# Two seven-product pairs instead of three, and splits with the weights' priority, in a two-layer fp32 block

## The chip, the core and the metric

The kernel runs on one core of a Trainium2 chip (trn2). The metric is device time in microseconds (us), median of the runs. PE is the matmul engine and PEld its weight loads, DVE the vector engine, ACT the scalar engine, POOL GpSimd, SP the engine that issues the DMAs here.

## The reference

Two layers over 256 rows of 2048 numbers, all in fp32. Each layer has a mixer (a gated linear recurrence, differential attention and latent attention side by side) and a feed-forward part. Only the second half of a layer matters here:

```
h = rmsnorm(x, g_ffn[l])
x = x + (silu(h @ w_gate[l]) * (h @ w_up[l])) @ w_down[l]
```

`w_gate` and `w_up` are 2048 x 5632, `w_down` is 5632 x 2048. The mixer's code is not touched.

## The kernel before, in words

Each product of fp32 matrices is made of three matmuls on numbers that are split in two: `hi` is the value rounded to the matmul's format (fp32r), `lo` the rest, and the product is hi x hi + hi x lo + lo x hi (`mm3`, lines 231 to 236). So each weight that arrives by DMA in a `wraw` buffer (6 of them, 512 KB each over 128 partitions) is first copied to `whi` by ACT (line 228) and then subtracted to `wlo` by DVE (line 229); of these there are 3 each.

The feed-forward part goes over 11 blocks f of 512 columns, in groups of 4, 4 and 3. For each f, `gate_up` computes gate and up for both halves of the 256 rows; there are 22 such calls in the two layers. After a group, its rows of `w_down` are multiplied in a stage of its own.

The 16 k-tiles of 128 rows are taken as 8 pairs. One pair is a 2 x 2 by 2 x 2 block product: two halves of the rows by two k-tiles, times two k-tiles by (gate, up). The first `NORD` pairs (5) are ordinary: 8 block products, 24 matmuls of 512 columns. The rest (3) use a scheme of the Strassen kind with 7 block products, 21 matmuls. For it, DVE makes sums of the weights, V and W (lines 340 to 343), in two more `wraw` buffers, and G, U, V and W are split into `arena` by ACT (lines 338, 339, 346, 348) and DVE (lines 344, 345, 347, 349). The arena holds two sets of such splits, at `p % 2 * SET`, so that one pair's are written while the other's are read. Sums of x for these pairs are made once a layer by `build_xS` into `xSh` and `xSl`.

PSUM has eight banks here: five of `acc`, three of `aux`. The seven-product part needs all five `acc` (C11, C22, C21, C12, P1) and all three `aux` (P5, P7, P6, lines 324 and 325).

When the last pair is done, DVE and ACT form silu(gate) * up in `sil` (lines 354 to 380). The down product needs it transposed and split. That is `hidden()`: two steps, each of four transposes on PE into an `aux` bank (line 393), a copy to `hTh` by ACT (line 399) and a subtraction to `hTl` by DVE (line 400). The steps are run by `tick()` beside the next call of `gate_up`, so its transposes stand in PE's order behind that call's third and fourth pair:

```
def hidden(sil=sil, h=h, lo=lo):
    yield 2
    for k in range(0, 4, 2):
        ps = transposed([0, 128, 256, 384], ...)
        split_scaled(fl(h[:, k:k + 2]), fl(lo[:, k:k + 2]), ps, None)
        yield
add(hidden())
```

PE runs in the order of the program text. The order on DVE, ACT and SP is made by a scheduler, which puts what stands under `tc.high_priority(offset=AHEAD)` ahead of the rest where both could go; the weights' splits, the sums and silu stand under it, `hidden()` does not. Every engine then works through its own row strictly in order.

Below, pair 0 to pair 7 are the eight pairs of a call.

Of the kernel before, what the change touches and what calls it, by code (L numbers as in the profile page):

```python
# [21 lines left out]
P = 128  # L22
D = 2048
T = 256
NT = 2
# [8 lines left out]
AHEAD = 100000  # L34
WIDTH = 2
STEPS = 2

NORD = 5
ARENA1, ARENA2 = 14504, 2816
MAGIC = 12582912.0  # L40
TWO_PI = 2.0 * math.pi
# [16 lines left out]
def body(ctx: ExitStack, tc: tile.TileContext, x_in, pos_in, pvec_in, lamv_in, cst_in, w_in, w_r, w_i, w_q_b,  # L58
# [26 lines left out]

    xSh = xt_p.tile([P, KD // 2 - NORD, 4, P], F32R, name="xSh")
    xSl = xt_p.tile([P, KD // 2 - NORD, 4, P], F32R, name="xSl")
    ar_p = pool("arena")
# [48 lines left out]
    A_ON = A_RG + 1024 + 1536  # L137
    A_DQ = A_QT

    SET = 7168  # L140
    A_SIL = ARENA1
    A_U = A_SIL + 1024

# [48 lines left out]
    def run(gen, ticks=None):  # L192
        for i, _ in enumerate(gen):
            if ticks is None or i < ticks:
                tick()
# [36 lines left out]
    def mm3(ps, a, b, start, stop):  # L232

        nc.tensor.matmul(ps, a[0], b[0], start=start, stop=False)  # L234
        nc.tensor.matmul(ps, a[0], b[1], start=False, stop=False)  # L235
        nc.tensor.matmul(ps, a[1], b[0], start=False, stop=stop)  # L236
# [61 lines left out]
    def gate_up(wg, wu, rs, sil):  # L298
# [3 lines left out]
        fl = lambda v: v.rearrange("p a b -> p (a b)")  # L302
# [7 lines left out]
        def xp(k, t):  # L310
            return xTh[:, k, t * P:(t + 1) * P], xTl[:, k, t * P:(t + 1) * P]

        for p in range(NORD):
            ks = (2 * p, 2 * p + 1)
            hl = [load_split(w[2 * p * P:(2 * p + 2) * P], 2, (512,)) for w in (wg, wu)]
            for s, t in ((0, 0), (1, 1), (0, 1), (1, 0)):
                hi, lo = hl[s]
                for j, k in enumerate(ks):
                    mm3(bank[s, t], xp(k, t), (hi[:, j], lo[:, j]), p == 0 and j == 0,
                        (s, t) == (1, 1) and p == NORD - 1 and j == 1)  # L320
            yield
# [4 lines left out]
        n = KD // 2  # L326
        for p in range(NORD, n):
            ks = (2 * p, 2 * p + 1)
            a = p % 2 * SET
            G, U = (load(w[2 * p * P:(2 * p + 2) * P], 2, (512,)).rearrange("p (a b) -> p a b", a=2)  # L330
                    for w in (wg, wu))
            V, W = (wraw_p.tile([P, CHUNK], F32, name="wraw").rearrange("p (a b) -> p a b", a=2) for _ in range(2))
            gh, gl = at(a, 2, 512), at(a + 1024, 2, 512)
            uh, ul = at(a + 2048, 512), at(a + 2560, 512)
            vh, vl = at(a + 3072, 2, 512), at(a + 4096, 2, 512)
            wh, wl = at(a + 5120, 2, 512), at(a + 6144, 2, 512)
            with tc.high_priority(offset=AHEAD):
                nc.scalar.copy(fl(gh), fl(G))  # L338
                nc.scalar.copy(uh, U[:, 1])
                tt(V[:, 0], U[:, 0], G[:, 0], ALU.subtract)  # L340
                tt(V[:, 1], U[:, 1], U[:, 0], ALU.subtract)  # L341
                tt(W[:, 0], U[:, 1], V[:, 0], ALU.subtract)  # L342
                tt(W[:, 1], G[:, 1], W[:, 0], ALU.subtract)  # L343
                tt(fl(gl), fl(G), f_(fl(gh)), ALU.subtract)  # L344
                tt(ul, U[:, 1], f_(uh), ALU.subtract)  # L345
                nc.scalar.copy(fl(vh), fl(V))  # L346
                tt(fl(vl), fl(V), f_(fl(vh)), ALU.subtract)
                nc.scalar.copy(fl(wh), fl(W))  # L348
                tt(fl(wl), fl(W), f_(fl(wh)), ALU.subtract)  # L349
            first, end = p == NORD, p == n - 1  # L350
            q = p - NORD
            S = [(xSh[:, q, i], xSl[:, q, i]) for i in range(4)]
            mm3(P1, xp(ks[0], 0), (gh[:, 0], gl[:, 0]), first, end)
            if end:
                with tc.high_priority(offset=AHEAD):
                    nc.scalar.copy(sil[1], P1)
            mm3(C11, xp(ks[1], 0), (gh[:, 1], gl[:, 1]), False, end)
            if end:
                with tc.high_priority(offset=AHEAD):
                    tt(sil[0], sil[1], C11, ALU.add)  # L360
                    nc.scalar.activation(sil[0], sil[0], AF.Silu, scale=rs[:, 0:1])
            mm3(C12, S[3], (uh, ul), False, end)
            mm3(P5, S[0], (vh[:, 0], vl[:, 0]), first, end)
            mm3(P7, S[2], (vh[:, 1], vl[:, 1]), first, end)
            mm3(P6, S[1], (wh[:, 0], wl[:, 0]), first, end)
            if end:
                with tc.high_priority(offset=AHEAD):
                    tt(u2, sil[1], P6, ALU.add)
                    tt(u3, u2, P7, ALU.add)
            mm3(C21, xp(ks[1], 1), (wh[:, 1], wl[:, 1]), False, end)  # L370
            if end:
                with tc.high_priority(offset=AHEAD):
                    tt(sil[1], u3, C21, ALU.add)
                    nc.scalar.activation(sil[1], sil[1], AF.Silu, scale=rs[:, 1:2])
                    tt(u2, u2, P5, ALU.add)
                    tt(u2, u2, C12, ALU.add)
                    tt(u3, u3, P5, ALU.add)
                    tt(u3, u3, o22, ALU.add)
                    for t, u in ((0, u2), (1, u3)):
                        nc.vector.scalar_tensor_tensor(sil[t], u, rs[:, t:t + 1], sil[t], ALU.mult, ALU.mult)  # L380
            yield
# [4 lines left out]
    def aux():  # L386
        return aux_p.tile([P, 512], F32, name="aux")

    def transposed(dsts, srcs):

        ps = aux()
        for d, s in zip(dsts, srcs):
            nc.tensor.transpose(ps[:, d:d + P], s, ident)  # L393
        return ps

    def split_scaled(hi, lo, src, g):

        if g is None:
            i = nc.scalar.copy(hi, src)
            nc.vector.tensor_tensor(lo, src, hi.bitcast(F32), ALU.subtract)  # L400
        else:
            i = nc.scalar.activation(hi, src, AF.Copy, scale=g)
            nc.vector.scalar_tensor_tensor(lo, src, g, hi.bitcast(F32), ALU.mult, ALU.subtract)  # L403
        return i
# [161 lines left out]
    def layer(l, rs):  # L566
# [3 lines left out]
        fl = lambda v: v.rearrange("p b t -> p (b t)")  # L570
# [231 lines left out]
        for i in range(4):  # L802
            h = ht_p.tile([P, 4, T], F32R, name="hTh")
            lo = ht_p.tile([P, 4, T], F32R, name="hTl")
            for j in range(4):

                k = (list(range(10, 16)) + list(range(6)) + list(range(6, 10)))[i * 4 + j]
# [148 lines left out]
        for f0, f1 in ((0, 4), (4, 8), (8, 11)):  # L956
            hT = []
            for f in range(f0, f1):
                sil = [at(A_SIL + t * 512, 512) for t in range(NT)]
                fs = slice(f * 512, (f + 1) * 512)  # L960
                run(gate_up(w_gate[l][:, fs], w_up[l][:, fs], rs[0], sil))
                h = ht_p.tile([P, 4, T], F32R, name="hTh")
                lo = ht_p.tile([P, 4, T], F32R, name="hTl")

                def hidden(sil=sil, h=h, lo=lo):
                    yield 2
                    for k in range(0, 4, 2):
                        ps = transposed([0, 128, 256, 384],
                                        [sil[t][:, (k + j) * P:(k + j + 1) * P] for j in range(2) for t in range(NT)])
                        split_scaled(fl(h[:, k:k + 2]), fl(lo[:, k:k + 2]), ps, None)  # L970
                        yield
                add(hidden())
                for j in range(4):
                    hT.append((h[:, j, :], lo[:, j, :]))
            last = f1 == 11
            if end and last:
                take(F32)
                gf = at(0, D)
                nc.sync.dma_start(gf, g_final.to_broadcast([P, D]))
            for cg in range(2):  # L980
                fin = end and last and cg == 1

                def ev(s, t, g, ps):
                    c = cg * 1024 + g * 512
                    nc.vector.tensor_tensor(x[:, t, c:c + 512], x[:, t, c:c + 512], ps, ALU.add)
                    if last:
                        sumsq(ss[:, t, cg * 2 + g:cg * 2 + g + 1], x[:, t, c:c + 512])
                    if end and last and cg == 0:
                        nc.vector.tensor_tensor(x[:, t, c:c + 512], x[:, t, c:c + 512], gf[:, c:c + 512], ALU.mult)
                    if fin and g == 1:  # L990
                        finish(t, ss, gf)
                run(gemm(lambda k: hT[k],
                         [(w_down[l][f0 * 512:f1 * 512, cg * 1024:(cg + 1) * 1024], [(0, 512), (512, 512)])],
                         [[k] for k in range(4 * (f1 - f0))], ev, last=3 if fin else 0))
                drain()
                if last and not end:
                    add(xT_steps("g_mix", l + 1, cg * 8, cg * 8 + 8))
# [62 lines left out]
```

## Time and profile before

| | |
|---|---|
| median of 3 runs | 2241.07 us (2236.26 to 2241.4) |
| the profiled execution | 2241.19 us, span 2239.4 us |
| mean granted clock of PE | 0.974 |
| PE busy | 2108.8 us (94%), 10104 matmuls |
| weight loads busy | 1761.2 us (79%) |
| DVE busy | 1545.2 us (69%) |
| ACT busy | 1136.2 us (51%) |
| HBM | 387.30 MB read, 174 GB/s over the span |

A matmul's end is modelled in the trace and reaches into the next one, so PE's pace is read from one start to the next. A wait is shown in brackets behind the instruction that waited, with what ended it.

### The profile page before, as it was taken

How to read it: one execution, taken by the hardware profiler on the slowest of the kernel's cores; microseconds unless marked ns; L12 is line 12 of the kernel's file. 1: busy time of each engine (PE TensorE's matmuls, PEld its weight loads, DVE VectorE, ACT ScalarE, POOL GpSimd, SP SyncE). 2: the span in 40 equal slices, each digit the busy share in tenths (PEclk: the TensorE clock that was granted, in tenths of full speed). 3: DMA queues.
4: the chain of work that ended last, by engine and by line, in shares of the span. 5: the costliest groups of instructions: out<-in, count | busy, mean ns of one | idle time of the engine just before them, and what ended most of it. 6: DMA issues, size and time to landing. Idle time of an engine off the chain costs nothing.

```text
span 2239.4 us, 27021 instructions
## 1 busy us (share of the span) xinstructions
PE 2108.8 (94%) x10104; PEld 1761.2 (79%) x10104; DVE 1545.2 (69%) x2115; ACT 1136.2 (51%) x1541; POOL 14.9 (1%) x32
## 2 busy tenths in 40 slices
PE   8999999888998889988999999998889988899888
PEld 8899887777887778877898898877778877788776
DVE  5775658777477774777566756587764877648775
ACT  5854656444354443444447545564543554434444
POOL 0000000000000000000000000000000000000000
PEclk9999999999999999999999999999999999999999
DMA  7564555545664555554565645654556645565553
GB/s 240 167 184 132 170 182 160 175 160 170 193 199 162 169 168 190 180 195 150 175 189 159 179 149 163 183 169 151 173 184 191 195 160 160 186 191 191 169 191 133
DMA packets 183220, 391.17 MB, mean 175 GB/s; under 512 B 18960, under 2 KB 36384, under 8 KB 182960
## 3 DMA queue, kind: packets, MB, share of 16 engines
q1 hardware_dynamic: 183040, 389.36, 54.9%
q8 instruction: 79, 1.29, 0.2%
q14 instruction: 53, 0.43, 0.1%
q0 software_dynamic: 48, 0.09, 0.0%
HBM read 387.30 MB, written 2.10 MB: 174 GB/s over the span
## 4 chain that ended last, share of the span: by engine, by line
PE 69%; DVE 17%; DMA 8%; issue 4%; ACT 2%; SPq 0%; DVEq 0%; POOLq 0%; POOL 0%; ACTq 0%
PE acc L235 20%; PE acc L234 20%; PE acc L236 20%; DMA wraw<-in_w_up 5%; DVE wlo L229 4%; PE aux L234 2%; DVE arena L344 2%; PE aux L235 2%; PE aux L236 2%; DVE arena L349 2%; ACT whi L228 1%; PE aux L393 1%; DVE arena L345 1%; DVE wraw L342 1%; DVE wraw L343 1%
## 5 line engine op out<-in xcount | busy, mean ns | idle before, releaser
L229 DVE TENSOR_TENSOR wlo<-wraw,whi 128x1024 fp32r<-128x1024 f32 (+2 forms) x608 | 716.1, 1182 | 451.5 <-ACT whi L228 446.2
L228 ACT CAST whi<-wraw 128x1024 fp32r<-128x1024 f32 (+2 forms) x608 | 618.7, 1019 | 728.4 <-PE acc L236 536.2
L235 PE MATMUL acc<-wlo,xTh 128*128 128x512 f32 (+1 forms) x1200 | 465.7, 388 | 11.3 <-DVE wlo L229 11.2
L234 PE MATMUL acc<-whi,xTh 128*128 128x512 f32 (+1 forms) x1200 | 471.1, 393 | 0.0
L236 PE MATMUL acc<-whi,xTl 128*128 128x512 f32 (+1 forms) x1200 | 463.5, 386 | 0.0
L234 PE MATMUL acc<-whi,hTh 128*128 128x512 f32 (+1 forms) x992 | 388.2, 391 | 0.0
L236 PE MATMUL acc<-whi,hTl 128*128 128x512 f32 (+1 forms) x992 | 384.7, 388 | 0.0
L235 PE MATMUL acc<-wlo,hTh 128*128 128x512 f32 (+1 forms) x992 | 384.4, 387 | 0.0
L235 PEld LDWEIGHTS acc<-wlo,xTh 128*128 128x128 f32 x1200 | 225.5, 188 | 65.7 <-DVE wlo L229 23.0
L234 PEld LDWEIGHTS acc<-whi,xTh 128*128 128x128 f32 x1200 | 225.4, 188 | 43.9 <-ACT whi L228 0.5
L236 PEld LDWEIGHTS acc<-whi,xTl 128*128 128x128 f32 x1200 | 225.3, 188 | 44.1
L234 PEld LDWEIGHTS acc<-whi,hTh 128*128 128x128 f32 x992 | 186.4, 188 | 37.8 <-issue 1.3
L236 PEld LDWEIGHTS acc<-whi,hTl 128*128 128x128 f32 x992 | 186.2, 188 | 37.9
L235 PEld LDWEIGHTS acc<-wlo,hTh 128*128 128x128 f32 x992 | 186.4, 188 | 36.4
L234 PE MATMUL aux<-arena,xSh 128*128 128x512 f32 x198 | 83.1, 420 | 100.6 <-DVE hTl L400 76.0
L234 PEld LDWEIGHTS aux<-arena,xSh 128*128 128x128 f32 x198 | 38.8, 196 | 114.1 <-ACT whi L228 93.2
L234 PE MATMUL acc<-xTh,whi 128*128 128x256 f32 x384 | 111.1, 289 | 1.7 <-ACT whi L228 1.0
L235 PE MATMUL acc<-xTl,whi 128*128 128x256 f32 x384 | 108.8, 283 | 1.6 <-DVE xTl L403 1.6
L236 PE MATMUL acc<-xTh,wlo 128*128 128x256 f32 x384 | 108.6, 283 | 0.5 <-DVE wlo L229 0.5
L346 ACT CAST arena<-wraw 128x1024 fp32r<-128x1024 f32 x66 | 69.3, 1049 | 47.6 <-DVE wraw L341 47.4
L344 DVE TENSOR_TENSOR arena<-wraw,arena 128x1024 fp32r<-128x1024 f32 x66 | 80.7, 1223 | 14.4 <-ACT arena L338 13.8
L348 ACT CAST arena<-wraw 128x1024 fp32r<-128x1024 f32 x66 | 69.4, 1051 | 36.3 <-DVE wraw L343 28.7
(230 smaller groups left out, 2614.5 us busy)
## 6 DMA issues: line engine op xcount, KB each, us to landing
wraw<-in_w_gate SPq DMA_DIRECT2D x176, 512.0 KB, 4.4
wraw<-in_w_up SPq DMA_DIRECT2D x176, 512.0 KB, 4.6
wraw<-in_w_down SPq DMA_DIRECT2D x176, 512.0 KB, 4.3
wraw<-in_w_out SPq DMA_DIRECT2D x64, 512.0 KB, 3.8
wraw<-in_w_in SPq DMA_DIRECT2D x48, 512.0 KB, 4.0
wraw<-in_w_in SPq DMA_DIRECT2D x48, 384.0 KB, 3.2
wraw<-in_w_in SPq DMA_DIRECT2D x32, 416.0 KB, 3.5
arena<-in_w_in SPq DMA_DIRECT2D x16, 384.0 KB, 7.4
```

The lines of the kernel that those rows point to most:

```text
L228: nc.scalar.copy(hi[:, :n], raw[:, :n])
L229: nc.vector.tensor_tensor(lo[:, :n], raw[:, :n], hi[:, :n].bitcast(F32), ALU.subtract)
L234: nc.tensor.matmul(ps, a[0], b[0], start=start, stop=False)
L235: nc.tensor.matmul(ps, a[0], b[1], start=False, stop=False)
L236: nc.tensor.matmul(ps, a[1], b[0], start=False, stop=stop)
L342: tt(W[:, 0], U[:, 1], V[:, 0], ALU.subtract)
L343: tt(W[:, 1], G[:, 1], W[:, 0], ALU.subtract)
L344: tt(fl(gl), fl(G), f_(fl(gh)), ALU.subtract)
L345: tt(ul, U[:, 1], f_(uh), ALU.subtract)
L346: nc.scalar.copy(fl(vh), fl(V))
L348: nc.scalar.copy(fl(wh), fl(W))
L349: tt(fl(wl), fl(W), f_(fl(wh)), ALU.subtract)
```

## The change

Three edits. `NORD` goes from 5 to 6, so 6 pairs are ordinary and 2 use seven products; `xSh` and `xSl` shrink from three entries to two. The transposes and splits of `hidden()` are issued under the weights' priority. The two sets in `arena` begin 64 elements (256 bytes) later.

```diff
-NORD = 5
+NORD = 6
...
-    SET = 7168
+    A_SET, SET = 64, 7168
...
         for p in range(NORD, n):
             ks = (2 * p, 2 * p + 1)
-            a = p % 2 * SET
+            a = A_SET + p % 2 * SET
...
                 def hidden(sil=sil, h=h, lo=lo):
                     yield 2
                     for k in range(0, 4, 2):
-                        ps = transposed([0, 128, 256, 384],
-                                        [sil[t][:, (k + j) * P:(k + j + 1) * P] for j in range(2) for t in range(NT)])
-                        split_scaled(fl(h[:, k:k + 2]), fl(lo[:, k:k + 2]), ps, None)
+                        with tc.high_priority(offset=AHEAD):
+                            ps = transposed([0, 128, 256, 384],
+                                            [sil[t][:, (k + j) * P:(k + j + 1) * P] for j in range(2)
+                                             for t in range(NT)])
+                            split_scaled(fl(h[:, k:k + 2]), fl(lo[:, k:k + 2]), ps, None)
                         yield
                 add(hidden())
```

How DVE's row changes is seen best in the third call of a group, which has the `hidden()` of the second beside it. The numbers in the names count buffers; they differ between the two programs. Before, at the end of the call, with the sums of pair 7 (`wraw_4294`, `wraw_4295`) and then the second `hTl`, behind which the next call's first weights follow:

```order
L340 TENSOR_TENSOR wraw_4294<-wraw_4292,wraw_4290 128x512
L341 TENSOR_TENSOR wraw_4294<-wraw_4292 128x512
L342 TENSOR_TENSOR wraw_4295<-wraw_4292,wraw_4294 128x512
L344 TENSOR_TENSOR arena_3292<-wraw_4290,arena_3292 128x1024
L343 TENSOR_TENSOR wraw_4295<-wraw_4290,wraw_4295 128x512
L345 TENSOR_TENSOR arena_3292<-wraw_4292,arena_3292 128x512
L347 TENSOR_TENSOR arena_3292<-wraw_4294,arena_3292 128x1024
L400 TENSOR_TENSOR hTl_4008<-aux_4164,hTh_4007 128x512
L229 TENSOR_TENSOR wlo_4351<-wraw_4348,whi_4350 128x1024
```

Now, in the middle of the call, with the split of pair 6's V (line 347), the second `hTl`, and then the first weights of pair 5 (`wlo_4196`):

```order
L347 TENSOR_TENSOR arena_3292<-wraw_4238,arena_3292 128x1024
L400 TENSOR_TENSOR hTl_3994<-aux_4150,hTh_3993 128x512
L229 TENSOR_TENSOR wlo_4196<-wraw_4193,whi_4195 128x1024
L342 TENSOR_TENSOR wraw_4239<-wraw_4236,wraw_4238 128x512
L343 TENSOR_TENSOR wraw_4239<-wraw_4234,wraw_4239 128x512
```

The second `hTl` stood behind all three pairs' sums but one split; it now stands inside those of the first of two.

The second place is the start of the first seven-product pair of that call on DVE. Before, it is pair 5 (sums in `wraw_4216`), and `wlo_4137` is the up weights of pair 3:

```order
L344 TENSOR_TENSOR arena_3292<-wraw_4212,arena_3292 128x1024
L340 TENSOR_TENSOR wraw_4216<-wraw_4214,wraw_4212 128x512
L341 TENSOR_TENSOR wraw_4216<-wraw_4214 128x512
L229 TENSOR_TENSOR wlo_4137<-wraw_4134,whi_4136 128x1024
L345 TENSOR_TENSOR arena_3292<-wraw_4214,arena_3292 128x512
```

Now it is pair 6 (sums in `wraw_4238`), with the first `hTl` ahead of it, and `wlo_4166` is the up weights of pair 4:

```order
L400 TENSOR_TENSOR hTl_3994<-aux_4107,hTh_3993 128x512
L344 TENSOR_TENSOR arena_3292<-wraw_4234,arena_3292 128x1024
L340 TENSOR_TENSOR wraw_4238<-wraw_4236,wraw_4234 128x512
L341 TENSOR_TENSOR wraw_4238<-wraw_4236 128x512
L345 TENSOR_TENSOR arena_3292<-wraw_4236,arena_3292 128x512
L229 TENSOR_TENSOR wlo_4166<-wraw_4163,whi_4165 128x1024
```

The split of line 345 has moved ahead of the weights' split.

## Rows read from the trace of the kernel before

**Rows 1.** Page, costliest groups: busy, mean ns | idle before, what ended it.
```profile
L234 PE MATMUL aux<-arena,xSh 128*128 128x512 f32 x198 | 83.1, 420 | 100.6 <-DVE hTl L400 76.0
```
**Rows 2.** Waits of PE: who for whom, us in total, times, longest.
```profile
PE aux L234 <- DVE hTl L400: 76.0, 12, 7.3
PE aux L234 <- ACT whi L228: 24.6, 4, 6.6
PE acc L235 <- DVE wlo L229: 11.2, 17, 1.2
```
**Rows 3.** Timeline of PE, one call: start us, us, instruction, idle before.
```profile
467.29 0.39 PE L236 MATMUL aux<-arena,xSl 128*128 128x512 f32 x1
474.88 0.77 PE L234 MATMUL aux<-arena,xSh 128*128 128x512 f32 x1 [7.21 <-DVE hTl L400]
...
479.20 0.39 PE L235 MATMUL acc<-arena,xTh 128*128 128x512 f32 x1
```
**Rows 4.** Timeline of ACT, the same call.
```profile
461.44 0.58 ACT L399 CAST hTh<-aux 128x512 fp32r<-128x512 f32 x1
```
**Rows 5.** Timeline of DVE, the same call.
```profile
451.71 0.69 DVE L340 TENSOR_TENSOR wraw<-wraw 128x512 f32<-128x512 f32 x1 [0.92 <-DMA wraw<-in_w_up]
...
452.92 1.22 DVE L229 TENSOR_TENSOR wlo<-wraw,whi 128x1024 fp32r<-128x1024 f32 x1
454.06 0.69 DVE L345 TENSOR_TENSOR arena<-wraw,arena 128x512 fp32r<-128x512 f32 x1
454.66 1.22 DVE L229 TENSOR_TENSOR wlo<-wraw,whi 128x1024 fp32r<-128x1024 f32 x1
...
474.05 0.69 DVE L400 TENSOR_TENSOR hTl<-aux,hTh 128x512 fp32r<-128x512 f32 x1
```
**Rows 6.** Windows: us, busy of PE, PEld, DVE, ACT, POOL, PEclk, DMA share, GB/s.
```profile
467.70:474.80 7.10, 0.00 (x0) 0.00 (x0) 7.10 (x11) 3.96 (x5) 0.00 (x0) 0.82 0.62 181
...
627.04:669.02 41.98, 41.78 (x184) 34.27 (x183) 34.43 (x39) 23.90 (x26) 0.00 (x0) 1.00 0.60 187
654.75:669.02 14.27, 14.27 (x64) 11.83 (x63) 13.57 (x17) 9.34 (x11) 0.00 (x0) 1.00 0.67 222
412.55:435.86 23.31, 17.18 (x65) 13.67 (x63) 15.43 (x19) 9.07 (x10) 0.00 (x0) 0.85 0.63 211
...
2141.28:2163.78 22.50, 16.50 (x64) 13.20 (x63) 15.29 (x19) 9.06 (x10) 0.00 (x0) 0.85 0.60 218
474.88:479.20 4.32, 4.32 (x11) 3.41 (x11) 3.61 (x4) 2.09 (x2) 0.00 (x0) 0.51 1.02 377
```
**Rows 7.** Groups by form, DVE and ACT: busy, mean ns of one.
```profile
L229 DVE TENSOR_TENSOR wlo<-wraw,whi 128x1024 fp32r<-128x1024 f32 x508 | 619.0, 1223 | 401.0 <-ACT whi L228 396.4
L344 DVE TENSOR_TENSOR arena<-wraw,arena 128x1024 fp32r<-128x1024 f32 x66 | 80.7, 1223 | 14.4 <-ACT arena L338 13.8
...
L340 DVE TENSOR_TENSOR wraw<-wraw 128x512 f32<-128x512 f32 x66 | 45.5, 690 | 22.4 <-DMA wraw<-in_w_up 22.2
...
L400 DVE TENSOR_TENSOR hTl<-aux,hTh 128x512 fp32r<-128x512 f32 x44 | 30.1, 685 | 0.0
...
L228 ACT CAST whi<-wraw 128x1024 fp32r<-128x1024 f32 x508 | 533.9, 1052 | 632.9 <-PE acc L236 500.9 <-issue 59.8 <-DMA wraw<-in_w_gate 21.1
...
L346 ACT CAST arena<-wraw 128x1024 fp32r<-128x1024 f32 x66 | 69.3, 1049 | 47.6 <-DVE wraw L341 47.4
```
**Rows 8.** Timeline of SP's queue, the same call.
```profile
447.96 0.37 SPq L212 DMA_DIRECT2D wraw<-in_w_up  x1
```
**Rows 9.** Timeline of PE, the same call and one without transposes.
```profile
454.25 0.44 PE L235 MATMUL acc<-wlo,xTh 128*128 128x512 f32 x1
...
644.73 0.39 PE L234 MATMUL acc<-whi,xTh 128*128 128x512 f32 x1
645.31 0.50 PE L235 MATMUL acc<-wlo,xTh 128*128 128x512 f32 x1 [0.20 <-DVE wlo L229]
```
**Rows 10.** Windows, the first call of layer 0.
```profile
342.00:390.00 48.00, 43.12 (x188) 33.55 (x187) 42.41 (x66) 31.31 (x43) 0.00 (x0) 1.00 0.52 163
```

## The prediction

> **What bounds the kernel now.** I read four views, each narrower than the last. The page's table of groups shows which PE group has idle time in front of it: nearly all of PE's idle time, 100.6 us, stands in front of one group, the first of three matmuls of a block product that writes an `aux` bank [rows 1]. The list of waits splits it: 12 waits of up to 7.3 us on `hTl` (line 400) and 4 of up to 6.6 us put down to `whi`; everything else that PE waits for is short, 17 waits on `wlo` with 11.2 us in all [rows 2]. So 16 waits. There are 22 calls of `gate_up`; the first of each of the six groups of f has no `hidden()` of an earlier call beside it, and 22 - 6 = 16. The four on `whi` are the same wait: same line, same place.
>
> The timelines show why. `aux` has three banks. `hidden()` of the call before takes two for its transposes, during the ordinary pairs; the first seven-product pair then wants three (P5, P7, P6). P6 gets the bank of the second transposes, which is free only when the copies to `hTh` and `hTl` have read it. In one such call PE stops after 467.29 and goes on at 474.88 [rows 3]. ACT had written `hTh` at 461.44 [rows 4]; DVE does `hTl` only at 474.05 [rows 5]. Between them DVE is never idle: 7.10 of 7.10 us [rows 6], on sums and splits of pairs 6 and 7, which have the weights' priority, while `hidden()` has none. The first block of rows in the change section says the same: `hTl_4008<-aux_4164` stands behind both pairs' sums. PE waits for a 0.69 us instruction in the wrong place of a queue.
>
> [...]
>
> **The change, part by part.**
>
> *The splits with priority.* They move in DVE's row from behind pair 7's sums to the middle of pair 6's; nothing is added. PE's order is the program's own and stays. What goes is the excess of the stretch of three seven-product pairs: 14.27 us without the wait, 23.31 in the first and 22.50 in the last of the 16 calls with it [rows 6]; all 16 lie between 22.0 and 23.7 and sum to 364.7. So 364.7 - 16 x 14.27 = 136.4 us. [...] Can the splits now hold up something else? Queued behind the second `hTl` on DVE is a `wlo` of pair 5 (`wlo_4196`). Its transposes are issued behind pair 3, `wlo_4196` waits for a buffer that pair 3 frees and is wanted only when pair 4 is done, 24 x 0.2265 = 5.4 us later. Two times 0.69 [rows 7] fits. The first `hTl` stands behind pair 4's first split, which itself waits for pair 2; its transposes run directly behind pair 2. I count no cost.
>
> *One pair with eight block products.* Three matmuls more per call: 22 x 3 x 0.2265 = 15.0 us, all on PE and so all on the path.
>
> [...]
>
> *What DVE and ACT lose and get.* A seven-product pair costs DVE five 512-wide instructions (0.69) and three 1024-wide (1.22), 7.1 us; an ordinary pair two of 1.22, 2.4 [rows 7]. A call without wait holds 34.43 us of DVE work in 41.98 [rows 6]; it comes to about 29.8 in 42.7, and 31.1 with the two `hTl`. DVE has the room on average; this is worth nothing on the path by itself, it is what makes the removed wait stay away: what is late next is only a matter of order.
>
> *The order around pair 4.* Here is the one new wait that I expect. DVE's order puts the sums of the first seven-product pair ahead of an ordinary split. Before, in the call shown, SP issues the up weights of pair 5 at 447.96 [rows 8], DVE starts on them at 451.71 after waiting for the landing, does two sums, and then the `wlo` that PE wants: 452.92 to 454.14 [rows 5]. PE uses it at 454.25 [rows 9], so it is just on time. In a call without transposes it is late: 0.20 recorded at 645.31 [rows 9], where the step from the matmul before is 0.58 in place of 0.2265, and the next one is long too, some 0.27 more than recorded. The second pair of blocks in the change section shows that now `L345` (from its start to the next is 0.60 [rows 5]) stands ahead of that `wlo` too. Everything else slides by one pair alike, with one more set of transposes on PE's side (about 0.3). So 0.3 late, 0.55 us of loss per call: 22 x 0.55 = 12.1 us. Bounds: 0 (the transposes cover it) and 1.2 + 0.27, the longest of the short waits, in every call: 32 us.
>
> *Fewer sums of x.* One of three `build_xS` per layer goes, in each layer's first call, which has short waits of its own: PE idles 48.00 - 43.12 = 4.9 us in its stretch [rows 10]. From 0 to -5 us a layer; I take 0, since the pair that stays first meets the same sums.
>
> *256 bytes.* Splits written into `arena` take 1223 ns on DVE and 1049 on ACT, those into `wlo` and `whi`, at quite other addresses, 1223 and 1052 [rows 7]; PE reads both at 0.2265. Nothing to gain, and two addresses with one speed give no reason for a loss: 0, within 3 ns an instruction.
>
> Sum, against the profiled execution (2241.2 us, span 2239.4; the median of the runs, 2241.07, is the same): 2241.2 - 136.4 + 15.0 + 12.1 = 2131.9, so **2132 us**. Its own range, by the bounds of the order term and a few us for the first calls: 2118 to 2145.
>
> **Rivals.**
>
> *No new wait at all.* The split stays in time everywhere and the first calls get shorter: 2241.2 - 136.4 + 15.0 = 2119.8, less up to 7: 2113 to 2120. For it: a call with transposes shows no wait there today. Against: one without does.
>
> *The up weights become the wait.* Without the 7 us pauses loads have less lead. If their landing is late by another us or two, each call loses 1.5 to 2.5 us at that same `wlo`: 2119.8 + 33 to 55 = 2153 to 2175. For it: `L340` waits for the up weights already. Against: a stretch without wait gets 222 GB/s [rows 6], and behind a wait 377 GB/s flow, so the engines have room.
>
> [...]
>
> *The wait only moves (slower than before).* If DVE, which works through its queue in order, stands at the head with an `hTl` whose transposes PE has not reached, pair 4's `wlo` behind it comes late, PE stops and pays wait and clock again, at pair 4 in place of P6: 16 times the same 8.5 us, and 15.0 for the added products, 2256 us. It decides from (136.4 - 15.0) / 22 = 5.5 us of new loss per call. The same time results if the edit of the priority does nothing, which the rows of the order exclude. Against it: by the order the transposes are issued one pair ahead of need.
>
> **How the numbers follow.** Forecast 0.62, no new wait 0.15, up weights 0.13, clock 0.03, wait moves 0.05, something between 2175 and 2235 0.02. A measurement of this kernel tells about 0.3% (7 us) from no change. All but the fifth are faster; of the fifth 0.02 I count as no change. Faster 0.94, same 0.02, slower 0.04. The range takes in the forecast, the case below it and most of the up-weights case: 2112 to 2168.
>
> **What would show it.** Right: PE's idle time in front of `aux` matmuls (100.6) is under 5 us; the stretch of now two seven-product pairs is 42 x 0.2265 = 9.5 us in all 22 calls; the mean clock rises from 0.974 to 0.99 or more; waits on `wlo` line 229 grow from 11.2 to some 15 to 25 us, most of them in pair 4. Groups of x66 become x44, and `wlo` 128x1024 x508 becomes x552. [...]

## The result and the profile after

The changed kernel takes 2113.55 us (median of 4 runs, 2111.89 to 2115.02) against 2239.12 for the kernel before in the same set of runs: ratio 0.944, 95% interval 0.9423 to 0.9456. Forecast were 2132 with a range from 2112 to 2168. So it came out 18 us below the forecast, where the rival "no new wait at all" stood (2113 to 2120). It lies outside the forecast's own range (2118 to 2145), and inside the full one only because that took in this rival.

The head of the page after: busy time of each engine, its share of the span, instructions.

```profile
span 2110.7 us, 27005 instructions
## 1 busy us (share of the span) xinstructions
PE 2087.3 (99%) x10170; PEld 1755.2 (83%) x10170; DVE 1455.8 (69%) x1973; ACT 1096.2 (52%) x1491; POOL 14.9 (1%) x32
```

PE's busy time fell from 2108.8 to 2087.3 us although it issues 66 matmuls more. Behind a wait of the kernel before, where the granted clock is 0.51 [rows 6], a matmul took 0.43 us from start to start:

```profile
475.44 0.63 PE L235 MATMUL aux<-arena,xSh 128*128 128x512 f32 x1
475.87 0.63 PE L236 MATMUL aux<-arena,xSl 128*128 128x512 f32 x1
```

Each of the 16 waits had at least five such steps behind it, and these are gone. The mean granted clock is 0.997, before 0.974.

PE's groups after, with idle time in front of them in the last column, answer to [rows 1]:

```profile
L234 PE MATMUL aux<-arena,xSh 128*128 128x512 f32 x132 | 51.3, 389 | 0.0
```

The 100.6 us are gone entirely. The waits of PE after (who for whom, us, times, longest) answer to [rows 2]:

```profile
PE acc L235 <- DVE wlo L229: 7.9, 11, 1.2
PE aux L872 <- ACT arena L552: 1.6, 2, 0.8
```

The waits on `wlo` did not grow from 11.2 to 15 to 25, as I expected; they shrank. The windows after, one call with a `hidden()` (ordinary part, then seven-product part), answer to [rows 6]; columns are us, busy PE, PEld, DVE, ACT, POOL, clock, DMA share, GB/s:

```profile
644.21:677.87 33.66, 33.66 (x154) 27.74 (x153) 25.43 (x30) 16.72 (x19) 0.00 (x0) 1.00 0.53 170
...
677.87:687.39 9.52, 9.52 (x44) 7.88 (x43) 9.52 (x12) 6.30 (x7) 0.00 (x0) 1.00 0.73 240
```

All 22 seven-product parts take 9.51 to 9.53 us, the 42 x 0.2265 of the forecast; 0.2265 us is one step where PE doesn't wait, 14.27 us for 63 matmuls [rows 6]. DVE is busy through all of that part in the call shown, and PE waits for it in none of the 22.

Where the time went, by the first matmul of each part in PE's timeline (profiled executions, 2241.19 and 2112.63 us):

| us | forecast | measured |
|---|---|---|
| waits on `aux` and their clock, 16 calls | -136.4 | -136.4 |
| three matmuls more in each of 22 calls | +15.0 | +15.1 |
| seven-product part of the two first calls of a layer (15.65 and 15.66 before) | 0 | -2.8 |
| short waits in the ordinary parts | +12.1 | -5.5 |
| sum | -109.3 | -129.6 (executions: -128.6) |

The fourth line is the difference of two sums: the ordinary parts of all calls take 637.0 us before and 751.0 after, 114.1 more, and one pair more in each is 22 x 24 x 0.2265 = 119.6. The second is that 119.6 less the 104.5 us by which 22 seven-product parts get shorter (14.27 to 9.52 each).

### The profile page after: what moved, and what is told of

Its sections match the earlier page's. It is cut to its first block, busy times and chain, and to the rows that moved or that the text cites. A ratio compares the mean times of both kernels' runs of the same rounds, so it can differ in the third digit from the quotient of the medians.

```text
span 2110.7 us, 27005 instructions
## 1 busy us (share of the span) xinstructions
PE 2087.3 (99%) x10170; PEld 1755.2 (83%) x10170; DVE 1455.8 (69%) x1973; ACT 1096.2 (52%) x1491; POOL 14.9 (1%) x32
## 4 chain that ended last, share of the span: by engine, by line
PE 93%; DVE 2%; DMA 2%; issue 1%; ACT 1%; SPq 0%; DVEq 0%; POOLq 0%; POOL 0%; ACTq 0%
PE acc L235 28%; PE acc L236 28%; PE acc L234 28%; PE aux L393 2%; PE aux L236 1%; PE aux L235 1%; PE aux L234 1%; DVE wlo L229 1%; DMA wraw<-in_w_up 1%; ACT whi L228 1%; PE aux L872 1%; DMA wraw<-in_w_gate 0%; PE aux L817 0%; PE aux L816 0%; DMA x<-in_x 0%
## 5 line engine op out<-in xcount | busy, mean ns | idle before, releaser
L229 DVE TENSOR_TENSOR wlo<-wraw,whi 128x1024 fp32r<-128x1024 f32 (+2 forms) x652 | 770.3, 1185 | 507.8 <-ACT whi L228 498.8
L228 ACT CAST whi<-wraw 128x1024 fp32r<-128x1024 f32 (+2 forms) x652 | 663.7, 1021 | 724.0 <-PE acc L236 582.4
L235 PE MATMUL acc<-wlo,xTh 128*128 128x512 f32 x1376 | 533.5, 388 | 8.1 <-DVE wlo L229 7.9
L234 PE MATMUL acc<-whi,xTh 128*128 128x512 f32 x1376 | 539.5, 392 | 0.0
L236 PE MATMUL acc<-whi,xTl 128*128 128x512 f32 x1376 | 531.7, 386 | 0.0
L235 PEld LDWEIGHTS acc<-wlo,xTh 128*128 128x128 f32 x1376 | 258.6, 188 | 66.2 <-DVE wlo L229 16.8
L234 PEld LDWEIGHTS acc<-xTh,whi 128*128 128x128 f32 x384 | 74.0, 193 | 4.2 <-ACT whi L228 1.5
L235 PEld LDWEIGHTS acc<-xTl,whi 128*128 128x128 f32 x384 | 74.1, 193 | 0.9 <-DVE xTl L403 0.8
L236 PEld LDWEIGHTS acc<-xTh,wlo 128*128 128x128 f32 x384 | 74.0, 193 | 0.7 <-DVE wlo L229 0.7
L344 DVE TENSOR_TENSOR arena<-wraw,arena 128x1024 fp32r<-128x1024 f32 x44 | 53.8, 1223 | 28.6 <-ACT arena L338 28.3
L338 ACT CAST arena<-wraw 128x1024 fp32r<-128x1024 f32 x44 | 46.3, 1052 | 36.1 <-DMA wraw<-in_w_gate 35.8
```

The costliest lines, as they stand in the source:

```text
L228: nc.scalar.copy(hi[:, :n], raw[:, :n])
L229: nc.vector.tensor_tensor(lo[:, :n], raw[:, :n], hi[:, :n].bitcast(F32), ALU.subtract)
```

## The experiments

**Each edit by itself.** The first question was which edit takes the wait away.

The priority alone:

```diff
-                        ps = transposed(...)
-                        split_scaled(...)
+                        with tc.high_priority(offset=AHEAD):
+                            ps = transposed(...)
+                            split_scaled(...)
```

> Three seven-product pairs as before, splits of hidden() with the weights' priority, no shift. Theory A (the late hTl alone makes the wait, the sixth ordinary pair only costs 15 us of PE): the 16 waits on aux are gone, every stretch of three seven-product pairs is 14.3 us, 2241 - 136 - 3 = about 2100 to 2108 us, faster than the changed kernel by 6 to 13. Rival B (three seven-product pairs need the pauses, DVE has no room without them: 35.8 of about 42 us per call): new waits of 0.5 to 2 us per call at wlo or at the arena splits, 2115 to 2150 us.

Measured: 2118.72 us (2116.89 to 2121.3), ratio to before 0.9451 (0.9437 to 0.9465). Six ordinary pairs alone:

```diff
-NORD = 5
+NORD = 6
```

> Two seven-product pairs, no priority, no shift. Theory A (the priority is what moves hTl): the waits on aux stay and the product is paid on top, about 2241 + 15 = 2256 us. Rival C (the scheduler places hTl early by itself once one more ordinary pair stands in front; its row has the second hTl behind the sum of line 342 of pair 6, ahead of pair 7): no wait on aux, the same time as the changed kernel within 5 us, 2109 to 2118 us.

Measured: 2114.9 us (2112.03 to 2116.1), ratio 0.9431 (0.9415 to 0.9447). So each edit alone takes the whole wait away. The same group of PE in the run with the priority alone (x198, three pairs) and in that with six pairs alone (x132):

```profile
L234 PE MATMUL aux<-arena,xSh 128*128 128x512 f32 x198 | 77.0, 389 | 0.0
```
```profile
L234 PE MATMUL aux<-arena,xSh 128*128 128x512 f32 x132 | 51.3, 389 | 0.0
```

With six pairs the scheduler places the second `hTl` early without being told to. In the run with six pairs alone it stands behind the third sum of pair 6, ahead of everything of pair 7:

```profile
670.47 0.69 DVE L342 TENSOR_TENSOR wraw<-wraw 128x512 f32<-128x512 f32 x1
671.07 0.68 DVE L400 TENSOR_TENSOR hTl<-aux,hTh 128x512 fp32r<-128x512 f32 x1
671.67 0.68 DVE L343 TENSOR_TENSOR wraw<-wraw 128x512 f32<-128x512 f32 x1
```

Theory A of the second run, 2256 us, fell; rival C held. What holds in both is that the place of `hTl` in DVE's row makes the wait: in the run with the priority alone, the work is that of the kernel before and the two `hTl` stand ahead of pair 6's sums. That priority is not what the changed kernel needed: with six pairs its effect is within what can be measured (2114.9 against 2113.0 without shift, below).

The priority alone also shows the other half: 15 us less work on PE, and still slower by some 6 us than the changed kernel without the shift in the same set of runs (2118.72 against 2112.97). Theory A of the first run, 2100 to 2108 us, fell with that. Its list of waits:

```profile
PE acc L235 <- DVE wlo L229: 16.0, 25, 1.2
PE acc L234 <- DVE arena L373: 2.9, 6, 1.0
PE aux L235 <- DVE arena L347: 2.2, 2, 1.1
```

Rival B of that run was right: without the long pauses DVE (37.92 us busy in a call of 43.29) has short delays in most calls. Where they are is plain in DVE's timeline: the split that PE waits for at 651.58 stands behind the end of silu(gate) * up, which DVE reaches late:

```profile
648.98 1.41 DVE L380 SCALAR_TENSOR_TENSOR arena<-arena,rs 128x512 f32<-128x512 f32 x2
650.31 2.35 DVE L229 TENSOR_TENSOR wlo<-wraw,whi 128x1024 fp32r<-128x1024 f32 x2
```
```profile
651.58 0.50 PE L235 MATMUL acc<-wlo,xTh 128*128 128x512 f32 x1 [0.71 <-DVE wlo L229]
```

**The 256 bytes**, alone, and taken out of the changed kernel (twice, in separate sets of runs):

```diff
-    SET = 7168
+    A_SET, SET = 64, 7168
```

> Before, with the sets in arena 256 bytes further. By the prediction nothing changes: 2235 to 2245 us, arena splits 1223 and 1049 ns, matmul steps 0.2265 us. Rival (the address matters): arena groups or matmul steps differ by over 1%, time off by over 10 us.

> The changed kernel with the sets at the old place in arena. By the prediction the same as the changed kernel: 2109 to 2118 us. Rival (the address matters): off by over 6 us.

> The changed kernel without the shift once more, beside the other counts of pairs on one chip: 2110 to 2116 us.

Measured: 2241.48 us with the shift alone, ratio 1.0003 (0.9993 to 1.0012); 2112.97 and 2112.45 us for the changed kernel without it. DVE's splits of line 344 in the run with the shift alone take 1222 ns, before 1223 [rows 7]:

```profile
L344 DVE TENSOR_TENSOR arena<-wraw,arena 128x1024 fp32r<-128x1024 f32 x66 | 80.7, 1222 | 15.4 <-ACT arena L338 15.4
```

The shift does nothing to the time that these runs could tell.

**How many pairs.** One seven-product pair, and four:

```diff
-NORD = 6
+NORD = 7     # the other run: 4, and without the shift
```

> Seven ordinary pairs and one seven-product pair, the rest as in the changed kernel. Theory: only PE's three matmuls per call are left to change, +15.0 us on 2113 and up to 5 us fewer short waits: 2123 to 2129 us. Rival (DVE still holds PE up with two seven-product pairs): 2118 us or less.

> Four ordinary and four seven-product pairs, splits with priority, no shift. If PE alone counted: 15 us less than with three, 2119 - 15 = 2104 us. Theory B (DVE is what the third and fourth seven-product pair run into: 35.8 + 4.7 = 40.5 us of DVE work in a call of 41.8): the waits grow by more than the product saves, 2120 to 2170 us, with waits of PE on arena splits as well as on wlo.

Measured: 2138.0 us with one (2136.7 to 2139.15), 2139.84 with four (2138.5 to 2142.78). The first is a miss by some 10 us, and its rival missed too: I had priced the product alone. The waits of that run, and one of them:

```profile
PE acc L235 <- DVE wlo L229: 17.2, 23, 1.4
```
```profile
677.44 0.50 PE L235 MATMUL acc<-wlo,xTh 128*128 128x512 f32 x1 [1.06 <-DVE wlo L229]
```

DVE's timeline of that run in front of it:

```profile
671.36 1.23 DVE L344 TENSOR_TENSOR arena<-wraw,arena 128x1024 fp32r<-128x1024 f32 x1 [1.51 <-ACT arena L338]
672.50 0.69 DVE L400 TENSOR_TENSOR hTl<-aux,hTh 128x512 fp32r<-128x512 f32 x1
673.10 1.22 DVE L229 TENSOR_TENSOR wlo<-wraw,whi 128x1024 fp32r<-128x1024 f32 x1
674.35 0.69 DVE L340 TENSOR_TENSOR wraw<-wraw 128x512 f32<-128x512 f32 x1
674.96 0.69 DVE L341 TENSOR_TENSOR wraw<-wraw 128x512 f32<-128x512 f32 x1
675.56 0.69 DVE L345 TENSOR_TENSOR arena<-wraw,arena 128x512 fp32r<-128x512 f32 x1
676.16 1.22 DVE L229 TENSOR_TENSOR wlo<-wraw,whi 128x1024 fp32r<-128x1024 f32 x1
```

The last four lines are the order that the forecast priced at 0.55 us a call: two sums and `L345` ahead of the split that PE wants. All 16 calls with a `hidden()` have it, and PE waits 0.54 to 1.40 us there, 0.82 on average. But DVE also comes late to the sums: `L344` has waited for ACT, and an `hTl` and one more split stand in between. No run took these two apart. The first calls of a group have the order of before, `L345` behind the split, and wait 0.24 to 0.38 us, about as before. In the changed kernel the 16 calls have the same four lines, and 14 of them don't wait. The next section says what is known of why.

With four, theory B held: DVE is busy 42.55 of 44.10 us in a call, and PE's waits on it grow to 27.9 us on `wlo` and 10.9 at line 373:

```profile
694.08:738.18 44.10, 42.56 (x189) 34.27 (x188) 42.55 (x54) 26.08 (x31) 0.00 (x0) 1.00 0.60 193
```

**What the clock has of the wait.** Behind the wait at 474.88, 11 matmuls take 4.32 us at a granted clock of 0.51 [rows 6]; 11 steps of 0.2265 are 2.49, which is 1.83 us less. The kernel before, with matmuls of zeros on PE in the place of the wait; DVE's row is as before:

```diff
+            if first:
+                for _ in range(fill):      # 26 in the 16 calls that wait, else 0
+                    nc.tensor.matmul(P7, warm[:, 0:P], warm, start=False, stop=False)
             mm3(P6, S[1], (wh[:, 0], wl[:, 0]), first, end)
```

> Before, with 26 matmuls of zeros (bf16, 512 columns, added to P7's bank) in PE's row ahead of P6's first use in the 16 calls that wait; DVE's row stays as it was. They add nothing to the result and fill some 5.6 to 5.9 us of each wait. Theory (each wait costs its length and, apart from that, 1.83 us of slow clock behind it): the clock stays high, the waits that are left are 0.1 to 1.6 us, 2241 - 16 x 1.83 = 2212, so 2206 to 2216 us. Rival (zeros do not hold the clock, or the slow clock belongs to something else in that stretch): 2236 to 2245 us.

Measured: 2208.99 us, ratio 0.9864 (0.9848 to 0.9881), 30.7 us less than before by medians. The chip does more, and is faster by 1.9 us for each of 16 waits; 1.83 was read from the row [rows 6]. The mean granted clock is 0.998. Behind one of the filled waits the clock is 1.00, where it was 0.51 [rows 6]:

```profile
470.71:475.00 4.29, 4.29 (x19) 3.54 (x20) 3.73 (x4) 2.00 (x2) 0.00 (x0) 1.00 1.03 388
```

What is left of the wait:

```profile
PE aux L234 <- DVE hTl L403: 5.1, 13, 1.0
...
PE aux L234 <- ACT whi L228: 1.9, 3, 1.1
```

So the 136 us were some 105 of waiting and 31 that go with the slow clock behind it. In the profiled executions the seven-product parts lose 34.6 us (453.1 to 418.5), so the second share is 31 to 35.

**A version that beats both**, the priority alone and the changed kernel. The last three DVE instructions of silu(gate) * up are issued behind the second weights' split of the next call's second pair, with three seven-product pairs and the priority:

```diff
-                    tt(u3, u3, o22, ALU.add)
-                    for t, u in ((0, u2), (1, u3)):
-                        nc.vector.scalar_tensor_tensor(sil[t], u, rs[:, t:t + 1], sil[t], ALU.mult, ALU.mult)
+                def tail():
+                    with tc.high_priority(offset=AHEAD), tc.issue_after(last_lo[0].ins):
+                        ...          # the same three
+                tails.append(tail)
...
-                    yield 2
+                    yield 1
+                    tails.pop()()
+                    yield 1
```

> Three seven-product pairs with priority, and the last three DVE instructions of silu(gate) * up of a call issued behind the second weights' split of the next call's second pair. Theory: in the run with the priority alone PE waits 13 times for just that split, 0.2 to 1.2 us and 0.27 more each; these go, 2119 - 14 = 2102 to 2108 us, faster than the changed kernel. Rival (DVE has no room at all there, the wait moves to the next split): 2115 us or more.

> The run with the late tail, with six ordinary pairs and two seven-product pairs in place of five and three. Theory (with two seven-product pairs the split behind the tail is in time already, so the late tail has nothing to give, and the third seven-product pair is worth 15 us less its waits): 2109 to 2116 us, as the changed kernel. Rival (the late tail helps here as well): 2106 us or less.

Measured: 2106.15 us with three seven-product pairs (2103.59 to 2107.24), ratio to before 0.9399 (0.9383 to 0.9415); 2112.48 with two, as the changed kernel. Both theories held. The first is 6 us below the changed kernel without shift in the same set of runs (2112.45, 2111.09 to 2115.42). In its timeline of DVE the split now stands ahead of the tail (its lines are two to five further down):

```profile
646.95 0.68 DVE L378 TENSOR_TENSOR arena<-arena,acc 128x512 f32<-128x512 f32 x1
648.46 1.22 DVE L231 TENSOR_TENSOR wlo<-wraw,whi 128x1024 fp32r<-128x1024 f32 x1 [0.83 <-ACT whi L230]
649.60 0.68 DVE L383 TENSOR_TENSOR arena<-arena 128x512 f32<-128x512 f32 x1
```

It waits for ACT, no longer behind DVE's own row. Left are 7.4 us on `wlo` over 12 waits, most of it in the first two calls of a layer, and 2.9 over 6 at line 375, where the down stage wants an `acc` bank.

## Why the prediction was right, and where it was not

*The wait and its price: right.* The stretch without wait, 14.27 us, was the right measure; all 22 calls now run at that pace, and the run with the zeros bears out that some of the loss goes with the clock and not with the waiting.

*Which edit removes it: wrong in part.* The forecast put the whole 136.4 us under the priority and took six pairs for a pure cost of 15 us. The order of the six pairs alone was not looked at; in it `hTl` is early without priority. That the forecast of the whole change was not hurt by this is luck: both edits were made together. By its own terms, six pairs alone would have been forecast at 2256 us, and it is 2115.

*The product: right.* 15.1 us. The 0.2265 us a matmul that it was made from, 14.27 us over 63 [rows 6], is 9.52 over 42 = 0.2267 after the change. The weight loads, for which the sum has no term, run beside the matmuls: PEld is busy for 7.88 us of a part of 9.52 that is full of matmuls, before for 11.83 of 14.27 [rows 6].

*The order around pair 4: the term that failed.* It was taken at +12.1 us; the ordinary parts lost 5.5 us of waits instead. It fails in three ways. First, it was priced in all 22 calls, but the order that it is about was read from a call with a `hidden()`, and only the 16 calls that have one show it. In the first calls of a group `L345` stays behind the split, as before the change; one of the four:

```profile
884.23 0.69 DVE L340 TENSOR_TENSOR wraw<-wraw 128x512 f32<-128x512 f32 x1 [0.62 <-DMA wraw<-in_w_up]
884.84 0.68 DVE L341 TENSOR_TENSOR wraw<-wraw 128x512 f32<-128x512 f32 x1
885.45 1.22 DVE L229 TENSOR_TENSOR wlo<-wraw,whi 128x1024 fp32r<-128x1024 f32 x1
886.58 0.69 DVE L345 TENSOR_TENSOR arena<-wraw,arena 128x512 fp32r<-128x512 f32 x1
```

Three of the four record a wait at this split, 0.74, 0.16 and 0.26 us; before, all four did, 0.20 to 0.35. That is the old wait and not a new one.

Second, in 14 of the 16 calls that have the new order the split is in time. The forecast's lower bound, "the transposes cover it", is what is seen there. Four transposes stand in PE's row right behind pair 3. PE's timeline after:

```profile
666.46 0.60 PE L393 MATMUL aux<-ident,arena 128*128 128x128 f32 x4
666.81 0.48 PE L234 MATMUL acc<-whi,xTh 128*128 128x512 f32 x1
...
668.52 0.42 PE L235 MATMUL acc<-wlo,xTh 128*128 128x512 f32 x1
```

and DVE's:

```profile
665.35 0.69 DVE L340 TENSOR_TENSOR wraw<-wraw 128x512 f32<-128x512 f32 x1 [0.57 <-DMA wraw<-in_w_up]
...
667.16 1.22 DVE L229 TENSOR_TENSOR wlo<-wraw,whi 128x1024 fp32r<-128x1024 f32 x1
```

The split is done at 668.38 and used at 668.52. I had given the one set of transposes that comes in addition 0.3 us; from the transposes' start to the seventh matmul behind them is 668.28 - 666.46 = 1.82 in place of 1.36, so it takes 0.46. With the 0.11 by which the split was early before (454.14 against 454.25), which I had left out of the sum, that is 0.57 of the 0.60 that `L345` costs. So the cover was mis-sized. That it is what keeps the split in time is argued from these sums; no run moved the transposes alone. With seven pairs the nearest set stands one pair ahead of the split's pair, and all 16 calls wait, but there DVE is late for other reasons too. The price of 0.55 us a call is seen by itself in no run.

Third, and worth most, the kernel before had a loss that I didn't count: a call that follows one without wait, the second of each group, had an ordinary part of 29.0 to 29.7 us in place of 28.2, since the split behind the tail of silu(gate) * up came late; in the first group of a layer it was 31.4, where one more split, ahead of the tail, was late as well. These six calls alone give back 9.2 us after the change; two others, below, lose 2.5. In the kernel before one such call:

```profile
676.67 0.50 PE L235 MATMUL acc<-wlo,xTh 128*128 128x512 f32 x1 [0.46 <-DVE wlo L229]
```

The forecast would have had every call follow one without wait, and so should have asked whether all 22 pay it. They don't: with two seven-product pairs DVE has less work behind it. In the changed kernel it reaches line 373, where the tail begins to run, 1.04 us after the next call's first matmul (644.21):

```profile
645.25 0.69 DVE L373 TENSOR_TENSOR arena<-arena,acc 128x512 f32<-128x512 f32 x1
```

With three, in the run with the priority alone, it is 2.30 us after it (643.68), and the tail and the split behind it are late by the difference:

```profile
644.06 1.23 DVE L229 TENSOR_TENSOR wlo<-wraw,whi 128x1024 fp32r<-128x1024 f32 x1
645.20 0.68 DVE L369 TENSOR_TENSOR arena<-arena,aux 128x512 f32<-128x512 f32 x1
645.98 0.69 DVE L373 TENSOR_TENSOR arena<-arena,acc 128x512 f32<-128x512 f32 x1
```

The run with the late tail, which differs from that run only in this place, is 13 us faster (2106.15 against 2118.72).

*DVE's load: too low, without effect.* A call was put at 31.1 us of DVE work in 42.7. It is 34.95 in 43.18 (644.21 to 687.39), and 31.60 in 42.67 in a first call of a group (863.04 to 905.71), which was put at 29.8. The row that the sum began from is such a first call, into which no earlier call carries the end of its silu(gate) * up. DVE still has room. (The chances given do not add up by 0.01 either: by the rivals it is 0.95 for faster and 0.03 for slower.)

*The up weights: seen, in two calls.* At 447.76 DVE waits 1.83 us for them, and PE then 1.01 at 450.85; likewise 1.03 at 712.93. SP had issued them at 442.87: 4.9 us until DVE can start, where a call without wait has 3.6 (661.71 to 665.35).

```profile
447.76 0.69 DVE L340 TENSOR_TENSOR wraw<-wraw 128x512 f32<-128x512 f32 x1 [1.83 <-DMA wraw<-in_w_up]
```

So that rival is real and costs some 2.5 us in all, not 33. What makes those two landings late stays open.

*Short waits and the clock: right for these calls.* A chance of 0.03 stood for a loss by the clock behind short waits too. Calls with waits of about 1 us keep the clock at 1.00 (687.38 to 722.36, with the 1.03 in it):

```profile
687.38:722.36 34.98, 33.95 (x154) 27.74 (x152) 25.61 (x30) 16.67 (x19) 0.00 (x0) 1.00 0.53 175
```

So do all 22 calls of the changed kernel, with waits of up to 1.23 us. In the run with one seven-product pair, with 23 waits on `wlo` of up to 1.40 us and a mean clock of 0.997, the matmuls behind each of them are back at 0.22 to 0.24 us from start to start from the second step on. It is no rule: in the run with the late tail, in the first call of layer 0, PE waits 0.64 and then 1.24 us, and behind that the clock is 0.50 over 3.00 us:

```profile
355.40 0.76 PE L237 MATMUL acc<-wlo,xTh 128*128 128x512 f32 x1 [1.24 <-DVE wlo L231]
```
```profile
355.50:358.50 3.00, 3.00 (x7) 2.34 (x8) 3.00 (x6) 1.26 (x3) 0.00 (x0) 0.50 0.18 20
```

*256 bytes: right*, nothing.

## What to carry to other kernels

When a wait is traced to one short instruction in the wrong place of an engine's row, look at the row that each edit makes by itself before putting the gain under one of them: a scheduler may move the instruction for another reason. When a long wait is to be taken out, measure the stretches that follow an undisturbed one before it: with the same work every stretch becomes like them (the priority alone), with less work for the helper engine it need not (the changed kernel). Read an order of instructions in every kind of call that the price is multiplied by. In these runs the best number of cheaper products is the one at which the helper engine just fits beside PE (DVE 38 of 43 us), and there the order of a few instructions decided the last 13 us.

## What the runs showed of the hardware

Adding 26 matmuls of zeros to each of 16 waits made the kernel faster by 1.4% (2208.99 us). Behind the waits of 5.8 to 7.3 us the granted clock was lower (0.51 over 4.32 us in the row shown) and a matmul took 0.42 to 0.43 us from start to start for five steps or more, and behind the same stretch filled with zeros it was 1.00 over 4.29 us. In the changed kernel's 22 calls, with waits of up to 1.23 us, the clock stayed at 1.00; in the run with the late tail it was 0.50 over 3.00 us behind two waits of 0.64 and 1.24 us, one right behind the other.
